# One step of a hybrid attention layer on one core: modulation product, w_out loads, last gate and prompt moved

## The chip, the cores and the metric

The kernel runs on 1 core of one Trainium2 chip. The metric is device time in microseconds of one execution. Of the engines, TensorE (PE) multiplies, VectorE (DVE), ScalarE (ACT) and GpSimd (POOL) work on tiles, and SyncE (SP) issues most of the DMA transfers. Each engine takes its instructions in a fixed order.

## The reference

```python
def merge_out(o_a, g_a, o_b, g_b, w_out):
    return jnp.concatenate([o_a * jax.nn.silu(g_a), o_b * jax.nn.silu(g_b)], axis=-1) @ w_out
...
shift, scale, gate = modulation(c, w_mod[l], b_mod[l])      # silu(c) @ w_mod + b_mod, in thirds
h = rmsnorm(xs, norm_gain[l]) * (1.0 + scale) + shift
q_a, k_a, v_a, g_a, q_b, k_b, v_b, g_b = project(h, w_in[l], ...)
...                                                         # axial rotary positions on q and k
o_a = global_attn_latent(q_a, k_a, v_a, cache_k_a[:, l], cache_v_a[:, l])
o_b = window_attn_latent(q_b, k_b, v_b, cache_k_b[:, l], cache_v_b[:, l], sink_b[l])
xs = xs + gate * merge_out(o_a, g_a, o_b, g_b, w_out[l])
```

One layer, float32. There are 1024 latent tokens and 128 prompt tokens of width 1024. Mixer A is global attention (8 query heads, 2 key heads, head size 64) over 1024 latent and 128 cached keys; mixer B takes a window of 128 on either side, the cached keys and a sink. The prompt goes through the same weights with a modulation of its own and attends to itself alone. Outputs are both residual streams and the prompt's keys and values.

## The kernel before, in words

Nearly every product is made of float32 values split into a high and a low part, so that three fast products (high by high, high by low, low by high) stand for one exact one. The work goes through stages:

1. **Start.** Nine tiles of 128 tokens are loaded (`load_x`), normed (`norm`: square on ACT, then two small instructions for the inverse root), scaled on DVE (`scaled`), transposed on TensorE (`turned`, L432), modulated to h (ACT and DVE, `modulated`) and split. The modulation's rows are a product on TensorE for each of 8 slices j of w_mod (`modulate_rows`, L398), copied (L401), transposed (`modulate`, L407) and added up to a scale and a shift. `warm(n)` issues n dummy matmuls (L468) between real ones; the tuple `WARM` has the counts. Tiles 1 to 4 are turned first, into one bank, and the first gate products (L273, L274, L269) follow with weights split by `W_GA.split()` (L244, L246).
2. **Projections** of queries, keys, values and gates. Queries and gates go out to DRAM (`qd`, `gd`) and are read again per unit (`u_load`, `load_gate`). The last gate of mixer B is not made by the Silu table but by `put_quotient`, in four steps, each in a tick of its own from `QUOTIENT_AT`: exponential, logarithm, exponential (ACT), product (DVE).
3. **Attention.** The work is a list of units (token tile t, mixer m, key head g), 32 of latents and then 4 of the prompt (32 to 35). Each unit has one slot for each block of 128 keys (a prompt's unit is padded to two slots). In slot s the program issues `tick()` (what is due on the agenda), the scores of slot s, loads and other items due, some matmuls of the output projection from a queue (`outq`), and the values product of slot s - 3 (`LAG`). So the order of each engine's instructions is that in which the slots and ticks issue them; `in_order` fixes it.
4. **Ends of a unit.** Counted in ticks from its last values product: `inverse` (ACT, L1207 to L1210), `gated` (DVE L1219, from the bank of PSUM into one third of the tile `spare`, the third being the unit's number modulo 3; then POOL L1221 by the gate `sgl`), `parts` (ACT L1231 high part; POOL L1233 low part a tick later), and for mixer B the output products (L1266). The ticks are `END_AT`, `EDGE_END` (global units of the first and last latent tile), `PROMPT_END`. `gated` also sets `load_gate(i + 2)` on the agenda, `GATE_LATE` ticks later. The values product has two banks, the `sgl` tiles have two buffers.
5. **w_out** comes in 16 blocks of 128 x 512, each loaded and split in two. Blocks 0 to 10 come during the last gates (`WO_STEPS`), the last five during the attention (`WO_LATE`: block, slot of its load; three ticks later `split_wo` on ACT L1088 and POOL L1089). These five use the two buffers `yt`, which the last gate's quotient has before and the output's sums behind them.

Of the kernel before, what the change touches and what calls it, by code (L numbers as in the profile page):

```python
# [33 lines left out]
PROMPT_AT = 32  # L34
# [12 lines left out]
PH_DVE = 0  # L47
MX_END = 10
MX_LEAD = 3
QUOTIENT_AT = 8  # L50
EARLY_STEPS = 50
SPLIT_LAG = 2

WO_LATE = {12: 18, 13: 19, 11: 30, 14: 31, 15: 33}

WO_STEPS = ((0, 4, 4), (1, 5, 5), (2, 6), (3, 7), (4, 8, 6), (5, 9), (6, 11), (7, 12, 10), (8, 13), (9, 14), (10, 16))
TURN = 2
# [1 line left out]
PAD = 2  # L59
X_FROM = 1  # L60
SECOND_FROM = 5
WARM = (4, 3, 3, 5, 2, 7)
WIDE = 5
LOADLEAD = 5
OUTRATE = 2.5
# [6 lines left out]
GATE_LATE = 2  # L72
END_AT = (1, 4, 6, 9)
EDGE_END = (1, 3, 6, 9)
PROMPT_END = (2, 4, 5, 7)
QTS = 5
PROMPT_LEAD = 4
EX_AT = (2, 2, 5)
# [37 lines left out]
def hybrid_step(ctx, tc, x_prompt, x_sample, cache_k_a, cache_v_a, cache_k_b, cache_v_b,  # L116
# [17 lines left out]
    def later(n, f):  # L134

        agenda.setdefault(now[0] + n, []).append(f)
# [208 lines left out]
    with tc.tile_pool(name="st", bufs=2, side="right") as st:  # L345
# [85 lines left out]
        def turned(px, j, t):  # L431
            nc.tensor.transpose(px, xn[t][:, P * j : P * j + P], ident)  # L432
# [32 lines left out]
        def warm(n):  # L465

            for _ in range(n):
                nc.tensor.matmul(small[0], ident_b, ident_b.unsqueeze(1).to_broadcast([P, 4, P]), start=True, stop=True)  # L468
# [20 lines left out]
        for j in range(KT + 2):  # L489
            if j == 0:  # L490
                px = bank_tr("px0_1")
                norm(1, nc.vector)
                norm(2, nc.vector)
                conditions()
                for i in range(4):
                    if 0 < i < 3:
                        norm(2 + i, nc.vector)
                    scaled(1 + i, rx.pop(1 + i))
                    warm(WARM[i])
                    turned(px[:, P * i : P * i + P], 0, 1 + i)  # L500
                modulate_rows(0)
                W_GA.split()
                warm(WARM[4])
                modulate(0)
                modulated(px, 0, 1, 4, 0)
                warm(WARM[5])
                continue
            big_on, small_on = j <= KT, 2 <= j
            if j < KT:
                W_GA.split()  # L510
            if j == 1:
                load_wm(3)
                norm(5)
            if big_on:
                first_gates(0, j - 1, 0)
                first_gates(1, j - 1, 0)
            if j < KT:
                modulate_rows(j)
                if j + 3 < KT:
                    load_wm(j + 3)  # L520
                if X_FROM <= j < X_FROM + 3:
                    load_x(rest[j - X_FROM])
            if big_on:
                first_gates(0, j - 1, 1)
                first_gates(1, j - 1, 1)
            if j == KT:
                sg_tile.append(lambda n: st.tile([P, D], F32, name="xn1", bufs=1)[:, 0:512])
                put_gates(big[0], 0, 0, slice(0, 512), nc.sync)
            if j == 1:
                modulate(1)  # L530
                scaled(5, rx.pop(5))
                transposed(1, 1, 4, 0)
                norm(6)
                first_gates(2, 0)
                first_gates(3, 0)
            elif j == 2:
                scaled(6, rx.pop(6))
                px5 = bank_tr("px01_5")
                for i in range(4):
                    turned(px5[:, P * i : P * i + P], i // 2, 5 + i % 2)  # L540
                modulate(2)
                for i in range(2):
                    modulated(px5[:, 256 * i : 256 * i + 256], i, 5, 2, 0)
                first_gates(2, 1)
                transposed(2, 1, 4, 0)
                first_gates(3, 1)
                transposed(2, 5, 2, 0)
            else:
                if big_on:
                    first_gates(2, j - 1)  # L550
                if j < KT:
                    modulate(j)
                    transposed(j, 1, 4, 0)
                if big_on:
                    first_gates(3, j - 1)
                if j < KT:
                    transposed(j, 5, 2 if j < WIDE else 4, 0)
            if X_FROM + 1 < j <= X_FROM + 4:
                t = rest[j - X_FROM - 2]
                scaled(t, rx.pop(t))  # L560
            if X_FROM < j <= X_FROM + 3:
                norm(rest[j - X_FROM - 1])
            for ch in range(4):
                if small_on:
                    next_gates(ch, j - 2)
                if ch % 2 or j >= KT:
                    more()
            if KT - 2 <= j < KT:
                raw = st.tile([P, KT, 2, P], F32, tag="wm", name=f"raw_qa{j}", bufs=3).rearrange(
                    "p (k a) s n -> p k (a s n)", a=2)  # L570
                k0 = 4 * (j - KT + 2)
                c0, n = W_QA.cols[0]
                nc.sync.dma_start(
                    raw, w_in[P * k0 : P * k0 + 512, c0 : c0 + n].rearrange("(k p) n -> p k n", p=P))
                W_QA.raw += [raw[:, k] for k in range(4)]
# [48 lines left out]
    with tc.tile_pool(name="qt", bufs=2, side="right") as qt:  # L624
# [89 lines left out]
        for m in range(2):  # L714
            w, nxt = ((W_QA, W_QB), (W_QB, W_KV))[m]
            ts = list(range(1, NT)) + [0]
            for t in ts:
# [3 lines left out]
                if (m, t) in ((0, ts[-2]), (1, ts[GATE_AT[0]])):  # L721
                    n = len(wg) // 2
# [465 lines left out]
    def values(i, b, last, blk, ph, pl):  # L1188
        t, m, g = units[i]
        _, vh, vl = blk  # L1190
        if b == 0:
            pvb[i] = bank("C", f"pv{i}")
        pv = pvb[i]
        two = vh.rearrange("p s d -> p (s d)")
        nc.tensor.matmul(pv, two, ph, start=(b == 0), stop=False)  # L1195
        if m == 0:
            nc.tensor.matmul(pv[0:64, :], vl, ph, start=False, stop=False)  # L1197
        nc.tensor.matmul(pv, two, pl, start=False, stop=last)  # L1198
        if not last:
            return  # L1200

        v = {}

        def inverse():
            v["rs"] = w2.tile([64, 512], F32, tag="rs", name=f"rs{i}", bufs=1)
            if m == 1:
                nc.scalar.copy(v["rs"], pv[64:128, :])  # L1207
                return
            nc.scalar.activation(v["rs"], pv[64:128, :], AF.Ln)
            nc.scalar.activation(v["rs"], v["rs"], AF.Exp, scale=-1.0)  # L1210

        def gated():
            rs = v["rs"]
            o = 768 + 256 * (i % 3)
            of = spare[:, o : o + 256].rearrange("p (c n) -> p c n", c=2)
            pvv = pv[0:64, :].rearrange("p (c s n) -> p c s n", s=2, n=P)
            srv = rs.rearrange("p (c s n) -> p c s n", s=2, n=P)
            for s in range(2):
                nc.vector.tensor_tensor(of[64 * s : 64 * s + 64], pvv[:, :, s, :], srv[:, :, s, :],  # L1219
                                        op=ALU.add if m else ALU.mult)  # L1220
            nc.gpsimd.tensor_tensor(of, of, sgl.pop(i), op=ALU.mult)  # L1221
            later(GATE_LATE, lambda: load_gate(i + 2))
            v["of"] = of

        def parts():
            while held[0] == NOG:
                outq.pop(0)()
            held[0] += 1
            oh = ogp.tile([P, 2, P], F32R, tag="ogh", name=f"ogh{i}")
            ol = ogp.tile([P, 2, P], F32R, tag="ogl", name=f"ogl{i}")  # L1230
            nc.scalar.copy(oh, v["of"])  # L1231
            og[t, 2 * m + g] = oh, ol
            later(1, lambda: nc.gpsimd.tensor_tensor(ol, v["of"], oh, op=ALU.subtract))  # L1233

        ends = (EDGE_END if m == 0 and t in (1, NL) else END_AT) if t else PROMPT_END
        for n, f in zip(ends, (inverse, gated, parts)):
            later(n, f)
        if m == 1:
            later(ends[3], lambda: outq.extend(out_items(t, g)))
# [54 lines left out]
    for i, (t, m, g) in enumerate(units):  # L1294
        if i in EARLY:
            continue
        if m == 0:
            items, done = max_items(i)
            at, end = [start[i - 2] + a for a in (MX_AT if i > 2 else MX_FIRST)], start[i - 2] + MX_END
# [19 lines left out]
    for s in range(len(slots) + LAG + PROMPT_END[3]):  # L1319
        tick()  # L1320
        if s < len(slots):
            live.append((slots[s], slots[s] and scores(slots[s][0], slots[s][1], slots[s][3])))
        for n, at in WO_LATE.items():
            if s == at:
                load_wo(n, w2)
                later(3, lambda n=n: split_wo(n, True))
        for f in due.get(s, ()):
            f()
        rate = (OUTRATE if s < start[PROMPT_AT - 2] else LASTRATE) if s < start[PROMPT_AT] else PADRATE
        credit = min(credit + rate, 6.0) if outq else 0.0  # L1330
        while outq and credit >= 1.0:
            outq.pop(0)()
            credit -= 1.0
        if s >= LAG and live:
            slot, parts = live.pop(0)
            if slot:
                values(*slot, *parts)
# [65 lines left out]
```

## Time and profile before

| | |
|---|---|
| time, median of 3 runs | 711.9 us (711.27 to 711.98) |
| the profiled execution's own time | 711.62 us |
| its span, first to last instruction | 709.8 us |
| mean granted TensorE clock | 0.999 |
| TensorE busy | 694.6 us (98%) |
| VectorE busy | 454.4 us (64%) |
| ScalarE busy | 414.0 us (58%) |
| GpSimd busy | 335.7 us (47%) |

A row of a timeline has the start in us from the span's start, the duration in us (of the whole run of equal instructions where it ends in xN), the engine, the line of the kernel, the operation, out<-in by the names of tiles, the shapes, and in brackets how long the engine stood idle ahead of it and what released it. A row of the waits has engine, tile and line, what it waited for, the total in us, the number of times and the longest. TensorE's matmuls overlap: one of 512 columns is shown with about 0.4 us.

### The profile page before, as it was taken

The numbers are of one execution on the slowest core, as the hardware profiler recorded it, in microseconds if no ns is written. First come the engines' busy times: TensorE is split into PE (matmuls) and PEld (weight loads), VectorE is DVE, ScalarE is ACT, GpSimd is POOL, SyncE is SP. The second block draws the span as 40 slices with busy tenths as digits, with TensorE's granted clock in tenths as the row PEclk, the third lists the DMA queues.
The fourth block names the chain that finished last, engine by engine and source line by source line (L and its number), as shares of the span: only waits on it lengthen the run. The fifth ranks groups of instructions, "written<-read, shape, count | busy, mean of one in ns | idle before, by whom it ended". The sixth has DMA issues, their size and how long they took to land. (4 is left out here: it accounts for less than half of the span.)

```text
span 709.8 us, 10658 instructions
## 1 busy us (share of the span) xinstructions
PE 694.6 (98%) x3524; PEld 557.6 (79%) x3524; DVE 454.4 (64%) x1010; ACT 414.0 (58%) x835; POOL 335.7 (47%) x349
## 2 busy tenths in 40 slices
PE   6999999999999999999999999999999999999997
PEld 2778988877788889976778788888888888887775
DVE  3575247867577763566667577667676775776562
ACT  4546412421324441188877877787788778877860
POOL 2466023233223330255867655755575557555751
PEclk9999999999999999999999999999999999999999
DMA  9951381228234026422222122122221231212323
GB/s 346 399 192 65 115 303 75 91 104 282 105 127 125 3 74 185 142 78 87 67 91 82 32 82 74 48 80 61 82 72 41 68 89 45 83 53 89 91 80 121
DMA packets 53304, 78.58 MB, mean 111 GB/s; under 512 B 6584, under 2 KB 25464, under 8 KB 52352
## 3 DMA queue, kind: packets, MB, share of 16 engines
q1 hardware_dynamic: 45936, 66.92, 28.8%
q10 hardware_dynamic: 7312, 10.98, 4.1%
q8 instruction: 28, 0.46, 0.3%
q14 instruction: 28, 0.23, 0.1%
HBM read 58.69 MB, written 19.18 MB: 110 GB/s over the span
## 5 line engine op out<-in xcount | busy, mean ns | idle before, releaser
L1185 POOL TENSOR_TENSOR pl<-pe,ph 128x512 fp32r<-128x512 f32 x130 | 167.5, 1291 | 149.7 <-ACT ph L1181 70.2
L933 DVE TENSOR_REDUCE mx<-pmx 128x1 f32<-128x384 f32 x192 | 101.0, 552 | 59.4 <-PE pmx L932 58.2
L1177 ACT ACTIVATE pe<-st 128x512 f32<-128x512 f32 x146 | 86.7, 594 | 29.3 <-PE st L1175 28.8
L1181 ACT CAST ph<-pe 128x512 fp32r<-128x512 f32 x146 | 90.6, 621 | 4.9
L1195 PE MATMUL pv<-ph,v_hi 128*128 128x512 f32 x208 | 82.5, 397 | 1.5 <-DVE spare L1219 1.5
L1198 PE MATMUL pv<-pl,v_hi 128*128 128x512 f32 x208 | 82.4, 396 | 0.0
L1266 PE MATMUL po<-wo,ogh 128*128 128x512 f32 x216 | 73.1, 395 | 0.2 <-DVE yt L1275 0.2
L184 POOL TENSOR_TENSOR rs_q<-ms_q,mhalf 128x8 f32<-128x8 f32 x18 | 34.8, 1933 | 81.0 <-DVE ms_q L182 81.0
L993 DVE CUSTOM_DVE_ANT_0 sn<-sn,mask,nsink 128x512 f32<-128x512 f32 (+1 forms) x64 | 46.4, 724 | 38.8 <-PE sn L990 35.8
L932 PE MATMUL pmx<-kha,qt 128*128 128x384 f32 x192 | 61.7, 367 | 0.6 <-ACT pen L979 0.3
L1174 PE MATMUL st<-qt,kha 128*128 128x512 f32 x144 | 57.9, 402 | 0.8 <-DVE pl L1171 0.8
L1197 PE MATMUL pv<-ph,v_lo 128*64 128x512 f32 x146 | 57.7, 395 | 0.0
L1175 PE MATMUL st<-qb,kla 68*128 68x512 f32 x144 | 57.0, 396 | 0.0
L1198 PEld LDWEIGHTS pv<-pl,v_hi 128*128 128x128 f32 x208 | 39.2, 189 | 16.7 <-POOL pl L1185 0.2
L698 ACT CAST qo0q<-ptq 128x512 fp32r<-128x512 f32 x18 | 10.6, 587 | 65.8 <-PE ptq L695 59.9
L979 ACT ACTIVATE pen<-sn,nm 128x512 f32<-128x512 f32 (+2 forms) x72 | 44.9, 625 | 5.9 <-DVE nm L1006 2.7
L1170 ACT CAST ph<-st 128x512 fp32r<-128x512 f32 x62 | 36.4, 587 | 19.8 <-PE st L1169 19.0
L1195 PEld LDWEIGHTS pv<-ph,v_hi 128*128 128x128 f32 x208 | 39.3, 189 | 8.5 <-ACT ogh L1231 1.1
L1266 PEld LDWEIGHTS po<-wo,ogh 128*128 128x128 f32 x216 | 40.0, 188 | 6.8 <-DVE yt L1275 0.6
L1171 DVE TENSOR_TENSOR pl<-st,ph 128x512 fp32r<-128x512 f32 x62 | 42.4, 685 | 2.3 <-ACT ph L1170 1.7
L1266 PE MATMUL po<-wo,ogl 128*128 128x512 f32 x108 | 42.6, 394 | 0.0
L932 PEld LDWEIGHTS pmx<-kha,qt 128*128 128x128 f32 x192 | 35.5, 190 | 9.0 <-DVE mx L933 3.3
(230 smaller groups left out, 1699.9 us busy)
## 6 DMA issues: line engine op xcount, KB each, us to landing
qt<-qd SPq DMA_DIRECT2D x72, 128.0 KB, 2.9
wm<-in_w_mod_ss_dram SPq DMA_DIRECT2D x7, 1024.0 KB, 9.4
qd<-qo0q ACTq DMA_DIRECT2D x18, 256.0 KB, 2.4
sgl<-gd SPq DMA_DIRECT2D x36, 128.0 KB
out_dram<-yt SPq DMA_DIRECT2D x17, 256.0 KB, 2.0
xn<-in_x_sample_dram SPq DMA_DIRECT2D x8, 512.0 KB
wg<-in_w_mod_g_dram SPq DMA_DIRECT2D x4, 1024.0 KB, 8.7
wraw<-in_w_out_dram SPq DMA_DIRECT2D x16, 256.0 KB, 4.9
```

What stands on the lines that cost most here:

```text
L932: nc.tensor.matmul(pm[:, 0:384], lhs, kha[:, g, 3 * b : 3 * b + 3, :], start=True, stop=True)
L933: nc.vector.tensor_reduce(mx[:, h, b : b + 1], pm[:, 0:384], axis=AX.X, op=ALU.max)
L993: nc.vector.tensor_tensor_reduce(s, s, mask[:, m0 : m0 + n], -1.0, nsink[:, 4 * g + h : 4 * g + h + 1], op0=ALU.add, op1=ALU.min, accum_ou ...
L1174: nc.tensor.matmul(s, kh, qtile[i], start=True, stop=False)
L1175: nc.tensor.matmul(s, kl, qbtile[i], start=False, stop=True)
L1177: nc.scalar.activation(pe, s, AF.Exp)
L1181: nc.scalar.copy(ph, pe)
L1185: nc.gpsimd.tensor_tensor(pl, pe, ph, op=ALU.subtract)
L1195: nc.tensor.matmul(pv, two, ph, start=(b == 0), stop=False)
L1197: nc.tensor.matmul(pv[0:64, :], vl, ph, start=False, stop=False)
L1198: nc.tensor.matmul(pv, two, pl, start=False, stop=last)
L1266: nc.tensor.matmul(po[n], a, wo_parts[KT * n + k][lo], start=(k == KS[0] and p == 0), stop=(k == KS[-1] and p == 2))
```

## The change

- `modulate_rows(0)` is issued ahead of the fourth transpose (i == 3) and no longer behind it; the dummies go from (4, 3, 3, 5, 2, 7) to (7, 2, 3, 2, 2, 6).
- `norm(6)` is issued right behind `norm(5)`, ahead of the first gate products of j == 1, and no longer behind tile 1's second h write.
- The four steps of the last gate's quotient come one tick sooner.
- w_out's blocks 11 and 14 are loaded in slots 28 and 29 (30 and 31 before) and split three ticks later; block 15 is loaded in slot 32 (33) and split four ticks later, so in tick 36 as before. Blocks 12 and 13 are as they were.
- All four steps at a prompt unit's end come one tick sooner, and the gate loads of units 32 to 35 one tick behind `gated` and not two.

```diff
-QUOTIENT_AT = 8
+QUOTIENT_AT = 7
...
-WO_LATE = {12: 18, 13: 19, 11: 30, 14: 31, 15: 33}
+WO_LATE = {12: (18, 3), 13: (19, 3), 11: (28, 3), 14: (29, 3), 15: (32, 4)}
...
-WARM = (4, 3, 3, 5, 2, 7)
+WARM = (7, 2, 3, 2, 2, 6)
...
-PROMPT_END = (2, 4, 5, 7)
+PROMPT_END = (1, 3, 4, 6)
...
                     scaled(1 + i, rx.pop(1 + i))
                     warm(WARM[i])
+                    if i == 3:
+                        modulate_rows(0)
                     turned(px[:, P * i : P * i + P], 0, 1 + i)
-                modulate_rows(0)
                 W_GA.split()
                 warm(WARM[4])
                 modulate(0)
...
                 norm(5)
+                norm(6)
...
                 transposed(1, 1, 4, 0)
-                norm(6)
...
-            later(GATE_LATE, lambda: load_gate(i + 2))
+            later(GATE_LATE if i + 2 < PROMPT_AT else 1, lambda: load_gate(i + 2))
...
-        for n, at in WO_LATE.items():
+        for n, (at, wait) in WO_LATE.items():
             if s == at:
                 load_wo(n, w2)
-                later(3, lambda n=n: split_wo(n, True))
+                later(wait, lambda n=n: split_wo(n, True))
```

## The prediction, on record before the changed kernel ran

> **What bounds the kernel now.** I read the page's busy shares first, then TensorE's waits, then the timelines of the places where TensorE waits, and last those of the engines that release it.
>
> ```profile
> span 709.8 us, 10658 instructions
> PE 694.6 (98%) x3524; PEld 557.6 (79%) x3524; DVE 454.4 (64%) x1010; ACT 414.0 (58%) x835; POOL 335.7 (47%) x349
> ```
>
> TensorE (PE) is busy for 694.6 of 709.8 us; no other engine is over 64%. So a change is worth only what it takes from, or adds to, the places where TensorE's stream of matmuls stands still. Its own waits say where these are:
>
> ```profile
> PE pg_s L468 <- DVE ident_b L349: 5.3, 1, 5.3
> PE px L432 <- DVE xn L418: 1.6, 2, 1.1
> PE pv L1195 <- DVE spare L1219: 1.5, 2, 0.8
> ```
>
> The first 5.3 us wait for the identity, which the change leaves alone. The second is the start (token tiles not yet scaled), the third the end (prompt). These lists leave out one thing: in the first 17 us TensorE is busy with dummies, which count as work here and are none. The gain of an earlier start is read from when the first real product begins, not from idle time.
>
> **The start: modulation product ahead of the fourth transpose, other dummies, norm(6) sooner.** Rows of TensorE, then the scaling of the fourth tile on VectorE (DVE), then ScalarE (ACT), then the DMA rate in slices of 1.5 us from 0 to 60 us:
>
> ```profile
> 8.50 1.49 PE L468 MATMUL pg_s<-ident_b 128*128 128x512 bf16 x3
> 9.78 0.42 PE L432 MATMUL px<-ident,xn 128*128 128x128 f32 x1
> ...
> 13.13 1.07 PE L398 MATMUL pm<-wm,sil 128*32 128x256 f32 x16
> ...
> 14.75 0.44 PE L407 MATMUL pm<-ident,mrows 128*128 128x128 f32 x2
> 15.03 1.67 PE L468 MATMUL pg_s<-ident_b 128*128 128x512 bf16 x7
> 16.78 0.50 PE L273 MATMUL pg_f<-h,whiga 128*128 128x512 f32 x1
> ...
> 25.05 0.55 PE L432 MATMUL px<-ident,xn 128*128 128x128 f32 x3 [0.51 <-DVE xn L418]
> ...
> 32.42 0.38 PE L407 MATMUL pm<-ident,mrows 128*128 128x128 f32 x2
> ```
>
> ```profile
> 10.95 0.75 DVE L418 TENSOR_SCALAR xn<-xn,rsx 128x1024 f32<-128x1024 f32 x1 [0.44 <-POOL rsx L428]
> ```
>
> ```profile
> 12.27 0.62 ACT L244 CAST whiga<-rawga 128x512 fp32r<-128x512 f32 x1 [2.63 <-DMA rawga<-in_w_in_dram]
> ...
> 20.75 0.78 ACT L447 ACTIVATE h<-px,b_col,a_mod 128x512 fp32r<-128x512 f32 x1 [2.46 <-DVE b_col L413]
> ...
> 29.13 1.06 ACT L424 ACTIVATE sq<-xn 128x1024 bf16<-128x1024 f32 x1 [0.61 <-DMA xn<-in_x_sample_dram]
> 30.18 0.60 ACT L244 CAST whiga<-rawga 128x512 fp32r<-128x512 f32 x1
> ...
> 31.29 0.37 ACT L401 COPY mrows<-pm 128x256 f32<-128x256 f32 x1 [0.50 <-PE pm L398]
> ```
>
> ```profile
> GB/s 0 200 416 397 421 287 320 434 426 401 415 451 412 407 442 437 437 362 438 429 401 227 388 401 377 96 273 386 137 14 191 404 102 0 23 343 333 11 0 0
> ```
>
> A dummy takes about 0.43 us early (three from 8.50 to 9.78) and 0.25 us later (seven from 15.03 to 16.78): the clock comes up near 12 us. Seven dummies from 5.27 at 0.43 us end at 8.26, so the gap ahead of the first transpose closes and TensorE is busy without a break from 5.27. I take it that the faster pitch comes by about 9.5 us. The third tile is scaled 0.44 us ahead of the row of 10.95; its transpose is done near 10.8, two dummies near 11.3, and the 16 instructions of the product (1.07 us) begin. Their weight's second half must be there: rawga's first tile, 256 KB behind it in SyncE's queue, lands at 12.25 or so; at some 420 GB/s that is 0.6 us later, so the half lands near 11.6 and the product ends near 12.2, against 14.2 before. The fourth tile is scaled at 11.70; its transpose and two dummies fit while DVE copies the rows. The transposes of 14.75 come at 12.95, the first gate product of 16.78 at 15.0: **-1.8 us**. The two dummies fewer (24 to 22) are inside that.
>
> What is late next? norm(6) moves on ACT from behind the h write of 20.75 to ahead of it: a square of 1.06 us, as at 29.13, and a short read. Its x6 stands behind rawga, 1 MB of wm, rawga and x5: 2.36 MB from 12.25 at about 430 GB/s is 17.8 us, so the norm holds ACT until 19.0, when the write is wanted at 18.95: 0.1 us lost, -1.7. Its two small POOL instructions are moved past nothing. In return the wait of 0.51 us at 25.05 is covered: -1.7 to -1.9. Then the gain meets a landing: at 29.13 ACT waited for x7, and behind it in ACT's order stand the weight cast of 30.18 and the row copy of 31.29. SyncE's order of loads is unchanged and the rate row shows the queue full up to there, so x7 comes no sooner. The copy can follow the cast at 30.8, ends at 31.15, and the transposes of 32.42 come at 31.2: **-1.2 us**, which I take; ends: -1.8 (x7 a little sooner) and -0.4 (clock late). By the Trainium skill, "DMA: Bandwidth & Descriptors", section on queues, rings and completion order, each engine consumes one queue's descriptors in ring order, so x7 could not overtake; by it the sum stays at -1.2 and the -1.8 is out. The trace's landing at 29.1 agrees.
>
> **The last gate's quotient a tick sooner.** ACT and TensorE at that place:
>
> ```profile
> 318.77 0.52 ACT L316 ACTIVATE quotient<-quotient 128x384 f32<-128x384 f32 x1
> ```
>
> ```profile
> 321.17 0.23 PE L951 MATMUL ptm<-ident_r,m_nat 128*4 128x128 f32 x1 [0.16 <-DVE mx L933]
> ```
>
> Three ACT instructions, one DVE product and one store by SyncE move one slot up. On DVE the product now comes ahead of the small maxima of the slot before, where it has idle time; the reductions that TensorE waits for stand behind it in DVE's order and come about 0.2 us sooner, and the wait at 321.17 shrinks: **-0.2 us** (0.2 either way at the ends: on ACT an exponential is half a us later, three slots ahead of its use).
>
> **The late w_out loads.** SyncE, ACT, POOL, DVE, TensorE, and of the chain that ended last the output products, for the pitch:
>
> ```profile
> 364.16 0.33 SPq L1072 DMA_DIRECT2D wraw<-in_w_out_dram  x1
> ```
>
> ```profile
> 367.19 0.62 ACT L1088 CAST wo_big<-wraw 128x512 fp32r<-128x512 f32 x1 [1.59 <-DMA wraw<-in_w_out_dram]
> ```
>
> ```profile
> 362.84 1.29 POOL L1089 TENSOR_TENSOR wo<-wraw,wo 128x512 fp32r<-128x512 f32 x1
> ```
>
> ```profile
> 369.74 0.69 DVE L1171 TENSOR_TENSOR pl<-st,ph 128x512 fp32r<-128x512 f32 x1 [1.35 <-ACT ph L1170]
> ```
>
> ```profile
> 370.58 0.47 PE L1174 MATMUL st<-qt,kha 128*128 128x512 f32 x1 [0.40 <-DVE pl L1171]
> ```
>
> ```profile
> 688.24 5.48 PE po L1266 x24
> ```
>
> Here is a chain to be had: w_out block 15 can't be loaded until POOL has split block 11 in the same buffer (362.84 + 1.29, issue at 364.16); it lands 3.0 us later, ACT stands 1.59 us for it, the cast of the scores behind it is late, DVE is late, and TensorE waits at 370.58 (0.40 us idle; at a pitch of 5.48 / 24 = 0.23 the matmul before, 0.4 us long, would have been followed 0.16 sooner than its end, so some 0.55 is lost). Block 11 is now split two slots sooner, near 361.2; 15 is issued then, lands near 364.4, and its split, in the same slot as before, finds it there. The wait goes: **-0.55 us**. Two ACT casts (0.62 each) and POOL splits (1.29 each) come into slots 31 and 32; ACT had gaps there, and POOL's splits of the exponentials, pushed by 1.3 to 2.2 us, still come about 1 us ahead of their matmuls. Ends: -0.6 and +0.2.
>
> **The prompt's steps and its gate loads a tick sooner.** TensorE, ACT, POOL, DVE at the end:
>
> ```profile
> 684.68 0.47 PE L1266 MATMUL po<-wo_big,ogl 128*128 128x512 f32 x1
> 685.92 0.47 PE L1195 MATMUL pv<-ph,v_hi 128*128 128x512 f32 x1 [0.77 <-DVE spare L1219]
> ...
> 687.54 0.47 PE L1195 MATMUL pv<-ph,v_hi 128*128 128x512 f32 x1 [0.69 <-DVE spare L1219]
> ```
>
> ```profile
> 682.05 0.60 ACT L1177 ACTIVATE pe<-st 128x512 f32<-128x512 f32 x1 [0.63 <-PE st L1175]
> ...
> 683.63 0.60 ACT L1209 ACTIVATE rs<-pv 64x512 f32<-64x512 f32 x1
> ```
>
> ```profile
> 683.38 1.29 POOL L1185 TENSOR_TENSOR pl<-pe,ph 128x512 fp32r<-128x512 f32 x1 [1.94 <-ACT ph L1181]
> 684.62 0.74 POOL L1221 TENSOR_TENSOR spare<-spare,sgl 128x256 f32<-128x256 f32 x1
> 685.31 0.73 POOL L1233 TENSOR_TENSOR ogl<-spare,ogh 128x256 fp32r<-128x256 f32 x1
> ...
> 687.71 0.74 POOL L1221 TENSOR_TENSOR spare<-spare,sgl 128x256 f32<-128x256 f32 x1 [0.97 <-DMA sgl<-gd]
> 688.41 1.43 POOL L1233 TENSOR_TENSOR ogl<-spare,ogh 128x256 fp32r<-128x256 f32 x2
> ```
>
> ```profile
> 685.80 0.69 DVE L1171 TENSOR_TENSOR pl<-st,ph 128x512 fp32r<-128x512 f32 x1
> 686.55 0.85 DVE L1219 TENSOR_TENSOR spare<-pv,rs 64x256 f32<-64x256 f32 x2
> ```
>
> Unit 32's inverse (logarithm and exponential on ACT, 683.63) moves ahead of unit 34's exponential (682.05). It begins at 681.6, its result is there at 682.8, DVE reads unit 32's bank by 684.5, and the wait of 0.77 us at 685.92 goes. But TensorE then only reaches the next wait sooner: unit 35's product needs unit 33's bank, read at 686.55. What sets that read? Unit 34's exponential is 0.8 us later, and with it POOL's 683.38 and, in order behind it, the gate product of unit 31 (684.62, now 685.4 to 686.2). Unit 32's gate product (0.74 too), a tick sooner, now stands ahead of unit 30's low part (685.31), which so ends near 687.55 in place of 686.05. Unit 33's read writes the third of "spare" that unit 30's low part still reads (30 and 33 leave the same remainder by 3), so it goes from 686.55 to 687.6, and TensorE's 687.54 to 688.6: **+1.05 us**. Behind it stand only output products, so nothing takes it back. The unit 31 low part, now third behind unit 33's gate product (687.71, whose gate load followed the row of 684.62 and landed 2.3 us behind it, so not before 688.5 now), is ready near 690.7, just ahead of the ninth output product at 691.0. Ends: -0.2 (the low part still ends in time: pairing 685.80 + 0.69 with the read) and +1.2. The gate loads are alone in SyncE's queue there; a tick changes nothing.
>
> **Sum:** -1.2 - 0.2 - 0.55 + 1.05 = -0.9 us on the profiled 711.62 us (span 709.8): 710.7. The runs' median is 711.9, 0.3 above the profiled one: **711.0 us**.
>
> **Rivals.**
> 1. *The prompt's steps lose nothing.* If unit 30's low part stays ahead on POOL, the end gives -0.2 and the sum is -2.15: 709.75. For it: both waits at the end are on exactly the step that moves. Against it: the order on POOL follows from the ticks.
> 2. *x7 does not hold the start.* The -1.75 us reach the first gates whole: sum -1.45, 710.45. For it: ACT's wait there is only 0.61 us. Against it: the full queue.
> 3. *The middle does nothing*: quotient and w_out stay hidden or their waits go to the next in line: sum -0.15, 711.75.
> 4. *Slower: the clock comes up late.* There are now fewer dummies between the transposes. If the fast pitch is not there by 12.1 us, all up to the product run at 0.43: the third transpose at 11.2, two dummies to 12.1, the product at half speed to 14.1, transpose and two dummies to 15.3, against 14.75: +0.5 in place of -1.2. Sum +0.8: 712.7. It decides where the product starts on the slow clock; up at 12.1 as before, the start still gains 0.9. By the Trainium skill, "TensorE: Matmul & The Clock Gate", Parts 1 and 4, the clock is released after a busy window of some 3.4 us that runs free of the program, and transposes do not count as busy in the same way: by it the step could fall anywhere up to a window later, the case of this rival. The trace agrees only that the pitch changed near 12 us, after steady work from 8.2.
>
> **How the numbers follow.** Chances: as worked out 0.52 (711.0; its own range 710.3 to 711.7), rival 1 0.18, rival 2 0.10, rival 3 0.13, rival 4 0.07. A measurement tells about 0.2% (1.4 us) from no change: faster is below 710.5, slower above 713.3. Rival 1, half of rival 2 and a fifth of the first case (0.11) give faster 0.34; rival 4's upper part and an unforeseen wait 0.07 slower; the rest 0.59. The range, 709.4 to 712.7, goes from rival 1 to rival 4.
>
> **What would show it.** Start: first gate product at 15.0, ACT's square of x7 still at 29.1, the transposes at 31.2 behind it. Middle: no wait of TensorE near 369, ACT's cast of block 15 without a DMA wait. End: the first wait for "spare" gone, the second longer, with POOL's low part of unit 30 late ahead of it. The prediction is wrong if x7 lands with the shift, if the low parts keep their places on POOL, or if the product of 13.13 runs at the slow pitch.

## The result

| | median us | runs | ratio to before, 95% interval |
|---|---|---|---|
| before | 711.94 | 4 (711.27 to 712.39) | |
| after | 715.62 | 4 (714.89 to 716.33) | 1.0052 (1.0035 to 1.007) |

The change makes the kernel 3.7 us slower (2.5 to 5.0 by the interval); 711.0 was predicted, with a range up to 712.7. All of the loss arises in the last 30 us of the profile: one and the same values product of TensorE stands at 680.64 before and at 679.19 in the changed kernel, 1.45 us sooner, and yet the span is 713.2 us against 709.8. First the page of the changed kernel and TensorE's waits (total, times, longest):

```profile
span 713.2 us, 10654 instructions
PE 695.6 (98%) x3522; PEld 558.1 (78%) x3522; DVE 455.7 (64%) x1010; ACT 414.8 (58%) x835; POOL 334.8 (47%) x349
```

```profile
PE pv L1196 <- DVE spare L1220: 2.5, 1, 2.5
PE pv L1196 <- ACT ph L1182: 1.2, 1, 1.2
...
PE pv L1199 <- POOL pl L1186: 0.6, 1, 0.6
```

The two waits for `spare` (0.77 and 0.69 us) have become one of 2.5, and two waits for unit 34's exponential and its low part (`ph`, `pl`) are new. The lines are one further on than before from L499 on.

**The start** (timeline of the changed kernel, TensorE, then ScalarE):

```profile
11.26 1.07 PE L398 MATMUL pm<-wm,sil 128*32 128x256 f32 x16
...
15.26 0.50 PE L273 MATMUL pg_f<-h,whiga 128*128 128x512 f32 x1 [0.65 <-ACT h L447]
...
31.07 0.44 PE L407 MATMUL pm<-ident,mrows 128*128 128x128 f32 x2 [0.56 <-ACT mrows L401]
```

```profile
29.08 1.06 ACT L424 ACTIVATE sq<-xn 128x1024 bf16<-128x1024 f32 x1 [2.63 <-DMA xn<-in_x_sample_dram]
...
30.65 0.36 ACT L401 COPY mrows<-pm 128x256 f32<-128x256 f32 x1
```

The modulation product begins at 11.26, the first gate product comes 1.52 us sooner, x7 lands where it did, and the transposes behind it stand at 31.07 in place of 32.42: 1.35 us are gained there, and the instructions behind keep 1.3 us of it up to 300 us. In the windows of this profile the granted clock reads 1.00 from the first microsecond on, although a dummy takes 0.43 us up to about 10 us (seven in 3.17 us from 5.25); so for the start the pitch of the matmuls is the evidence of the clock, and not that column.

**The end** (timelines of ScalarE, POOL, VectorE and TensorE):

```profile
682.37 0.60 ACT L1210 ACTIVATE rs<-pv 64x512 f32<-64x512 f32 x1 [2.39 <-DVE spare L1220]
...
683.66 0.60 ACT L1178 ACTIVATE pe<-st 128x512 f32<-128x512 f32 x1
684.29 0.62 ACT L1182 CAST ph<-pe 128x512 fp32r<-128x512 f32 x1
```

```profile
684.98 1.28 POOL L1186 TENSOR_TENSOR pl<-pe,ph 128x512 fp32r<-128x512 f32 x1 [4.71 <-ACT ph L1182]
686.22 1.41 POOL L1222 TENSOR_TENSOR spare<-spare,sgl 128x256 f32<-128x256 f32 x2
687.59 0.73 POOL L1234 TENSOR_TENSOR ogl<-spare,ogh 128x256 fp32r<-128x256 f32 x1
```

```profile
681.40 0.86 DVE L1220 TENSOR_TENSOR spare<-pv,rs 64x256 f32<-64x256 f32 x2
...
688.35 0.85 DVE L1220 TENSOR_TENSOR spare<-pv,rs 64x256 f32<-64x256 f32 x2 [1.20 <-POOL ogl L1234]
```

```profile
683.30 0.48 PE L1267 MATMUL po<-wo_big,ogl 128*128 128x512 f32 x1
684.96 0.50 PE L1196 MATMUL pv<-ph,v_hi 128*128 128x512 f32 x1 [1.17 <-ACT ph L1182]
685.30 0.39 PE L1198 MATMUL pv<-ph,v_lo 128*64 128x512 f32 x1
686.31 0.50 PE L1199 MATMUL pv<-pl,v_hi 128*128 128x512 f32 x1 [0.62 <-POOL pl L1186]
689.34 0.71 PE L1196 MATMUL pv<-ph,v_hi 128*128 128x512 f32 x1 [2.53 <-DVE spare L1220]
```

Unit 32's inverse (682.37) is now first in ScalarE's order but stands 2.39 us: it writes the tile `rs`, of which there is one buffer, and that is free only when VectorE has read unit 31's reciprocals out of it (681.40 + 0.86 = 682.26). Behind it in order stand unit 34's exponential (683.66, 3.0 us later than 682.05 less 1.35) and its cast; POOL's low part waits for them, unit 31's and 32's gate products and unit 30's low part stand behind that, and VectorE's read of unit 33 writes the third of `spare` that unit 30's low part reads. And TensorE's clock falls (windows: us, TensorE busy, granted clock, DMA):

```profile
684.00:688.00 4.00, 1.23 (x3) 1.00 0.00 0
688.00:690.00 2.00, 0.66 (x2) 0.85 0.47 131
690.00:692.00 2.00, 2.00 (x7) 0.50 0.35 90
692.00:694.00 2.00, 2.00 (x9) 0.79 0.71 238
```

0.85 over 2 us is 0.6 us at half clock, 0.79 is 0.84 us: half clock from 689.4 to 692.84, 3.44 us. The eight matmuls in it follow at 0.43 us in place of 0.23, which costs 1.6 us. A wait costs the distance between two starts less the usual 0.23: 683.30 to 684.96, 685.30 to 686.31 and 686.31 to 689.34 give 1.43 + 0.78 + 2.80 = 5.0 us, a tenth more with the next matmul. The same sum for the changed kernel with the old ticks (a1 below; 683.43 to 684.71 and 685.25 to 686.33) is 1.05 + 0.85 = 1.9. So in these profiles the new ticks cost 3.2 us in waits and 1.6 in the clock, 4.8 together.

### The profile page after: what moved, and what is told of

It is laid out like the page before. It is cut to its first block, busy times and chain, and to the rows that moved or that the text cites. A ratio compares the mean times of both kernels' runs of the same rounds, so it can differ in the third digit from the quotient of the medians.

```text
span 713.2 us, 10654 instructions
## 1 busy us (share of the span) xinstructions
PE 695.6 (98%) x3522; PEld 558.1 (78%) x3522; DVE 455.7 (64%) x1010; ACT 414.8 (58%) x835; POOL 334.8 (47%) x349
```

## The experiments

| run | kernel | median us | ratio to before |
|---|---|---|---|
| a1 | after, old prompt ticks | 710.58 | 0.9977 (0.9967 to 0.9986) |
| a2 | before, new prompt ticks | 717.42 | 1.0073 (1.0057 to 1.0088) |
| a3 | after, only the inverse sooner | 714.37 | 1.0031 (1.0019 to 1.0044) |
| a4 | after, only the other three sooner | 713.19 | 1.0016 (1.0007 to 1.0025) |
| b1 | after, own room for `rs` | 712.94 | 1.0011 (1.0001 to 1.002) |
| b4 | b1, own room for unit 33's output | 710.97 | 0.9991 (0.9982 to 1.0) |
| b2 | after, 12 dummies in the gap | 713.58 | 1.0030 (1.0018 to 1.0043) |
| b3 | before, new start alone | 710.11 | 0.9976 (0.9967 to 0.9984) |
| c3 | before, new dummies alone | 710.83 | 0.9984 (0.9975 to 0.9993) |
| c4 | before, new order alone | 711.37 | 0.9993 (0.9983 to 1.0002) |
| c2 | b3 and the quotient | 710.33 | 0.9981 (0.9971 to 0.999) |
| c1 | b3 and w_out | 710.46 | 0.9980 (0.9971 to 0.9989) |
| d3 | b3, prompt's inverse sooner with room | 710.62 | 0.9983 (0.9974 to 0.9992) |
| d4 | d3, residual loads ahead of gate loads | 709.36 | 0.9967 (0.9954 to 0.9979) |

Before had a median between 711.8 and 712.1 in each set of runs, so medians of different sets are compared below to some 0.2 us at best. An interval of the ratio is about 0.002 wide, which is 1.4 us, and smaller differences are read from the places in the profiles.

### Whose loss is it: the prompt's ticks (a1 to a4)

```diff
-PROMPT_END = (1, 3, 4, 6)
+PROMPT_END = (2, 4, 5, 7)     # a1; a3: (1, 4, 5, 7); a4: (2, 3, 4, 6)
```

a2 is the kernel before with (1, 3, 4, 6) and the gate loads' tick.

> The changed kernel with the prompt's four steps at their old ticks (2, 4, 5, 7); the rest of the change stays, the tick of the prompt's gate loads too. Theory 1 (the prompt's steps lose all of it: unit 32's inverse stands on ScalarE for the one buffer of the reciprocals, and TensorE then falls to half its clock): 715.6 - 4.8 = about 710.4 to 710.8, with the two small waits for the third of spare back at 684.6 and 686.2 and all output products at 0.23 us. Theory 2 (the clock at the end falls because of the new dummies or an earlier start, and the ticks are innocent): 714 to 715.6, with slow matmuls near 689.

> The kernel before with the prompt's four steps a tick sooner and its gate loads a tick sooner, nothing else. Theory 1: +4.8, so 716.7 (715 where the clock holds). Theory 2: +1 (as predicted for the order on POOL alone), 713.

> The changed kernel with only the first of the four steps (the inverse) a tick sooner: 1, 4, 5, 7. Theory 1 (the inverse waits on ScalarE until unit 31's read frees the one buffer of the reciprocals): the wait of 2.4 us at rs stays, unit 34's exponential is late, about 712.4, up to 714 if the clock drops as well. Theory 2 (the order of the gate product and the low parts on POOL costs the time): no loss, 710.4.

> The changed kernel with the inverse at its old tick and the other three steps a tick sooner: 2, 3, 4, 6. Theory 1: ScalarE does not wait for rs, 710.4 or a little less. Theory 2: the low part of unit 30 stands behind the gate product of unit 32 on POOL, +0.75, 711.2 or more.

The prompt's ticks make the whole loss: without them the rest of the change is 1.5 us faster than before (a1), with nothing else they cost 5.3 (a2). The tick of the gate loads is in a1 too, so it isn't that. Of a2's surplus over the 4.8 the clock has a part: its windows

```profile
688.00:690.00 2.00, 0.54 (x1) 0.66 0.00 0
690.00:692.00 2.00, 0.64 (x2) 0.50 0.45 131
692.00:696.00 4.00, 4.00 (x12) 0.57 0.49 163
```

show half clock for 1.36 + 2 + 3.44 = 6.8 us, twice as long as in the changed kernel. But 2.7 us of it fall into the wait itself, which ends at 691.36; slow matmuls follow for 4.1 us in place of 3.5, which is some 0.3 us more. a3 keeps the wait for `rs`, as theory 1 said:

```profile
682.09 0.60 ACT L1210 ACTIVATE rs<-pv 64x512 f32<-64x512 f32 x1 [2.28 <-DVE spare L1220]
```

It comes out a little above the upper end that theory 1 gave (714.37 against 714), and the clock drops in it too. a4 has no such wait, so theory 1 expected 710.4; theory 2 said 711.2 or more from an addition of 0.75. 713.19 is far over the first and over twice that addition. Its ScalarE shows a third mechanism (first the two rows of a4, then the same copy in a1):

```profile
685.47 0.41 ACT L1232 CAST ogh<-spare 128x256 fp32r<-128x256 f32 x1 [1.13 <-POOL spare L1222]
685.90 0.58 ACT L1208 COPY rs<-pv 64x512 f32<-64x512 f32 x1
```

```profile
684.65 0.58 ACT L1208 COPY rs<-pv 64x512 f32<-64x512 f32 x1 [0.35 <-DVE spare L1220]
```

With `parts` a tick sooner and the inverse not, the high part of a gated tile, which waits for POOL's gate product, stands ahead of unit 33's copy on ScalarE. The copy is 1.25 us later, so is unit 33's read (686.58 against 685.34 on VectorE), and TensorE's second wait grows from 0.7 to 1.9. A further wait of 1.15 at 694.93 stands behind unit 35's read in VectorE's order. The order on POOL that theory 2 named is there too, but the low part of unit 30 ends at 686.13 and unit 33's copy at 686.48, so the copy decides. Moving steps together costs other things than moving them alone; a3 and a4 do not add up.

### The two shared buffers (b1, b4)

```diff
+            if t == 0 and m == 0:
+                if not room:
+                    room.append(qp2[0].tile([P, 4, 512], F32, tag="pen", name="room"))
+                v["rs"] = room[0][0:64, g, :]
+            else:
                 v["rs"] = w2.tile([64, 512], F32, tag="rs", name=f"rs{i}", bufs=1)
...
+            if i == PROMPT_AT + 1:                                       # b4 only
+                of = room[0][:, 2, 0:256].rearrange("p (c n) -> p c n", c=2)
```

(The expectation says units 32 and 33; the units with an inverse, whose reciprocals get the room, are 32 and 34.)

> The changed kernel, but the reciprocals of the prompt's units 32 and 33 go to a room of their own, so that unit 32's inverse need not wait until unit 31's read is done. Theory 1 (that wait is the greater part of the loss): the 2.4 us on ScalarE ahead of rs are gone, unit 34's exponential is 0.8 us late, what stays is near the +1.05 that was predicted, 711.5 to 711.8, and the clock holds. Theory 2 (the loss is the order on POOL): 715 or more as in the changed kernel.

> As the kernel with a room for the reciprocals of units 32 and 33, and unit 33's output tile in that room too, so that it need not wait until unit 30's low part is read. Theory 1 (the third of spare is what is left of the loss, as predicted): 0.3 to 0.8 under the kernel with the room alone, about 711. Theory 2 (other order on POOL, the low part of unit 31): no less than that kernel.

b1, timelines of ScalarE, VectorE and TensorE, then its windows:

```profile
680.70 0.60 ACT L1216 ACTIVATE room<-pv 64x512 f32<-64x512 f32 x1
...
681.99 0.60 ACT L1179 ACTIVATE pe<-st 128x512 f32<-128x512 f32 x1
```

```profile
686.70 0.85 DVE L1226 TENSOR_TENSOR spare<-pv,rs 64x256 f32<-64x256 f32 x2 [0.99 <-POOL ogl L1240]
```

```profile
684.71 0.45 PE L1200 MATMUL pv<-pl,v_hi 128*128 128x512 f32 x1
687.70 0.59 PE L1197 MATMUL pv<-ph,v_hi 128*128 128x512 f32 x1 [2.54 <-DVE spare L1226]
```

```profile
688.00:690.00 2.00, 2.00 (x6) 0.50 0.21 52
690.00:692.00 2.00, 2.00 (x7) 0.67 0.85 272
```

The wait on ScalarE is gone, and with it 2.7 us. b1 is what the prediction described: the first wait for `spare` gone, the second longer because unit 30's low part stands between. TensorE's stream loses 2.76 us at that place against 1.90 in a1, +0.9, where +1.05 was predicted. The rest, some 1.5 us between the medians, is the clock, which falls after this one wait too: half clock for 3.4 us by the windows. b4 takes the shared third of `spare` away, the longest wait falls to 1.4, the clock holds, and 2.0 more come back, not the 0.3 to 0.8 expected: the expectation left the clock out. That its "about 711" was met is luck, since it was counted from a time for b1 that was too low by more than a us. With both buffers out of the way the new ticks still gain nothing: b4 stands at 710.97, a1 with the old ticks at 710.58.

### The clock (b2)

```diff
+            if slot and slot[0] == NU - 1:
+                dummy = bank("A", "dummy")
+                for _ in range(12):
+                    nc.tensor.matmul(dummy, ident_b, ident_b.unsqueeze(1).to_broadcast([P, 4, P]), start=True,
+                                     stop=True)
```

> The changed kernel with 12 dummy products of 512 columns ahead of unit 35's values product, where TensorE stands for 2.5 us. Theory 1 (TensorE's clock falls to half because of the idle time in there, and that costs 1.5 to 1.7 us of the 4.8): the matmuls from 689.3 on keep a pitch of 0.23, about 714.0. Theory 2 (the clock falls for another reason, so idle time is not the cause): half speed stays, 715.6 or more.

```profile
688.00:690.00 2.00, 2.00 (x10) 1.00 0.46 131
690.00:692.00 2.00, 2.00 (x11) 1.00 0.25 69
```

Twelve matmuls that compute nothing make the kernel 2.0 us faster (713.58 against 715.62): the wait is as long as it was (686.51 to 689.55 between the two real matmuls, 686.31 to 689.34 without dummies), but the matmuls behind it keep their 0.23 us. So idle time is the cause of the low clock. How much is enough: in the profiled executions a wait of 2.54 us with nothing else (b1) was; 0.81 and 1.88 with three matmuls between (a4) were not, nor 1.4 (b4).

A profile is one execution, however, and the mean granted clock, which is on record for every run, says that runs of one kernel differ here. Five of a4's ten runs have 0.996 and no run of a1 or b3 is under 0.998, so in these five the clock very likely fell, though the profiled one (712.66, clock 0.999) shows nothing of it. Two of b1's ten runs have 1.000 (711.51 and 712.79), so there it very likely held in spite of the wait. The changed kernel's own runs are two at 0.998 (714.89 and 714.98, the profiled one) and two at 0.994 (716.27 and 716.33). So the clock's 1.6 us are the price in one execution and not a constant. What share of such a stretch must be idle is left open.

The Trainium skill, "TensorE: Matmul & The Clock Gate", Part 1, says that the clock is decided in free-running windows of about 3.4 us and halves after an idle one. The lengths agree: 3.44 us of half clock in the changed kernel, 6.8 in a2. Its rule that only gaps above some 3.4 us matter does not hold here: 2.54 us in b1 were enough.

### The start (b3, c3, c4)

b3 has only the start's part of the change; c3 only the dummies; c4 the order of product and norm with the old dummies.

> The kernel before with the changes at the start alone (modulation product ahead of the fourth transpose, the other dummies, norm 6 sooner). Theory 1 (the start's 1.3 us are kept through the whole kernel): 710.6. Theory 2 (they are lost at a later landing or wait): 711.9.

> The kernel before with the new dummies alone (7, 2, 3, 2, 2, 6 in place of 4, 3, 3, 5, 2, 7), the modulation product still behind the fourth transpose. Theory 1 (half of the start's gain is the clock that comes up sooner, half is the product that no longer waits for the fourth tile): the product begins near 12.2 in place of 13.13, the transposes at 32.42 come 0.5 to 1.3 sooner because the landing of x7 caps the rest, about 711.0. Theory 2 (the dummies give nothing without the new order): 711.9.

> The kernel before with the new order at the start alone (product ahead of the fourth transpose, norm 6 sooner), the old dummies. Theory 1: the clock comes up near 12 as before, the product begins near 12.1 behind five dummies that run slowly, 1.0 sooner than before, and x7 caps what is kept: 710.8 to 711.3. Theory 2 (without the early clock nothing is gained, the rival of the prediction): 711.9 or slower.

The modulation product of c3, then that of c4:

```profile
12.03 1.07 PE L398 MATMUL pm<-wm,sil 128*32 128x256 f32 x16
```

```profile
12.69 1.07 PE L398 MATMUL pm<-wm,sil 128*32 128x256 f32 x16
```

It began at 13.13 before and at 11.62 in b3. c3 lies near its expectation. c4 is just over its own: the five slow dummies took longer than allowed for, the product came 0.4 us sooner, not 1.0, and against before the time can't be told from no change. Yet in both profiles the transposes behind x7 come 1.1 us sooner (31.32 and 31.31 against 32.42), close to b3's 1.53, though the products differ by 0.7: x7 lands at 28.9 to 29.2 in all of these profiles and caps what is kept. So in these two executions either half brings most of what x7 lets through. They are the fastest of ten in both cases (709.91 and 710.23), though. By the medians of each set the dummies bring 1.0 us and the order 0.5, which may be nothing, and both together (b3) 1.9; how the gain divides stays open.

### The middle (c1, c2)

c1 adds `WO_LATE` of the change to b3, c2 `QUOTIENT_AT = 7`.

> The kernel before with the changes at the start and the late w_out loads; quotient and prompt as before. It tells the two changes of the middle apart. Theory 1 (the quotient made the new wait near 313, w_out the one near 364): the shift stays at -1.4 to -1.5 through 314 and 320, drops by 0.5 near 364, comes back by 0.4 to 0.5 at 370, so w_out is worth 0 to -0.2 and the time is 710.0 to 710.3. Theory 2 (the wait near 364 comes from the quotient's sooner maxima): no drop near 364, and -0.5 as predicted, 709.6.

> The kernel before with the changes at the start and the quotient a tick sooner, w_out and prompt as before. Theory 1 (the quotient's exponential stands ahead of a penalty on ScalarE, TensorE waits near 313, and the shorter wait at ptm gives back less): the shift falls by 0.35 to 0.4 at 314, 0.1 comes back by 320, so 0.25 is lost: 710.4. Theory 2 (as predicted, 0.2 gained): 709.9, no new wait near 313.

Both times stand within 0.35 us of b3's 710.11, which is within the intervals. The places differ, though. c2, ScalarE and TensorE:

```profile
311.88 0.48 ACT L310 ACTIVATE quotient<-pg 128x384 f32<-128x384 f32 x1
312.25 0.57 ACT L980 ACTIVATE pen<-sn,nm 128x384 f32<-128x384 f32 x1
```

```profile
312.97 0.45 PE L933 MATMUL pmx<-kha,qt 128*128 128x384 f32 x1 [0.18 <-ACT pen L980]
```

The quotient's exponential now stands ahead of a penalty that frees the bank of the next maxima: the shift against before falls from -1.52 to -1.16 at 314; 0.1 is back by 317, the wait at `ptm` near 321 (0.16 before) is gone, as predicted, and -1.44 is there again at 360, where b3 has -1.41. c1, VectorE, POOL, TensorE:

```profile
362.18 1.33 DVE L947 TENSOR_SCALAR m_nat<-m 128x4 fp32r<-128x4 f32 x1
363.43 0.55 DVE L934 TENSOR_REDUCE mx<-pmx 128x1 f32<-128x384 f32 x1
```

```profile
362.20 1.29 POOL L1186 TENSOR_TENSOR pl<-pe,ph 128x512 fp32r<-128x512 f32 x1
```

```profile
364.03 0.44 PE L933 MATMUL pmx<-kha,qt 128*128 128x384 f32 x1 [0.41 <-DVE mx L934]
```

A VectorE instruction on 128x4 took 1.33 us and ended 0.02 us behind POOL's. In b3 it took 0.51 (from 362.25), and ended 0.02 behind another POOL instruction, which ended at 362.74. w_out's splits, moved on POOL, put a long POOL instruction beside it; the maxima behind it are late and TensorE loses 0.57 at 364 and 0.1 at the next start. The wait at 370 goes as predicted and gives 0.65 back: against before nothing is left. Against b3 there was less to gain from the start: with the old loads the two matmuls at that place start 0.53 us apart in b3, 0.80 before, and 0.23 where nothing waits.

### A version that is faster than both (d3, d4)

d3 is b3 with the inverse a tick sooner, the rooms of b4, unit 33's read two ticks sooner, and its gate product and high part later, behind the low parts of units 31 and 32. d4 also issues the last image tile's residual loads earlier:

```diff
-PROMPT_END = (2, 4, 5, 7)
+PROMPT_END = (1, 4, 5, 7)
...
+        if i == PROMPT_AT + 1:
+            ends = (1, 2, 6, 7)
...
+            if i == PROMPT_AT + 1:
+                later(3, lambda: nc.gpsimd.tensor_tensor(of, of, sgl.pop(i), op=ALU.mult))
+            else:
                 nc.gpsimd.tensor_tensor(of, of, sgl.pop(i), op=ALU.mult)
...                                                                      # d4 only
-            if n == 0 and k == KS[4] and p == 0:
+            if n == 0 and k == KS[0 if t == NL else 4] and p == 0:
```

> The kernel before with the changes at the start, and of the prompt's steps only the inverse a tick sooner, with a room of its own for the reciprocals of units 32 and 34 and for unit 33's output tile; unit 33's read two ticks sooner, its gate product on POOL behind the low parts of units 31 and 32. Theory 1 (the two shared buffers are all that stood against the sooner steps, and the order on DVE and POOL is the rest): the idle time of TensorE between 683 and 689, 1.9 us in the kernel before, falls to 0.5 to 1.0, so 708.8 to 709.3. Theory 2 (something else holds unit 35's product): no gain over the start alone, 710.1 or more.

> The kernel with the inverse a tick sooner and a room of its own, and the two loads of the last image tile's residual rows (yt) put ahead of the prompt's gate loads in SyncE's queue. Theory 1 (there VectorE waited for yt because its load stood behind a gate load that waits for unit 33's gate product; TensorE lost 1.28 at 692.42): yt is there in time, the wait falls to the 0.3 that the kernel before shows, so 1.0 less than that kernel: 709.2 to 709.6. Theory 2 (the output products wait for something else there, the low parts or the store): 710.6 as without it.

d3's TensorE, VectorE and SyncE:

```profile
692.42 0.70 PE L1280 MATMUL po<-wo,ogh 128*128 128x512 f32 x2 [1.12 <-DVE yt L1289]
```

```profile
691.58 0.69 DVE L1289 TENSOR_TENSOR yt<-po,yt 128x512 f32<-128x512 f32 x1 [1.44 <-issue]
```

```profile
684.61 3.83 SPq L1157 DMA_DIRECT2D sgl<-gd  x3
688.49 0.93 SPq L1261 DMA_DIRECT2D yt<-in_x_sample_dram  x2
```

The waits of 1.9 us between 683 and 689 fell to 0.9, as theory 1 said (the longest left is 0.28 for unit 33's read), but 1.28 were lost at 692.42, so the time, 710.62, missed theory 1's 708.8 to 709.3 and is no better than b3's. Unit 33's later gate product holds a `sgl` buffer, SyncE waits for it with a gate load, and the residual rows (`yt`) stand behind that load, so VectorE had to wait for them. With those loads ahead (d4) SyncE issues them at 675.91, the loss at that place is 0.2, and 709.36 is 2.7 us under before. It is also 0.75 under b3, but the intervals of the two ratios overlap, so that part is likely and not sure.

## Why the prediction was wrong

- **The start** (-1.2): right, in the mechanism as well as the size. Product at 11.26 (11.3 predicted), first gate product at 15.26 (15.0), x7 at 29.08 (29.1), transposes at 31.07 (31.2): -1.35. Rival 2 is out: x7 landed within 0.3 us of the same time in five profiles. That, and not the order of the queue on which the prediction leaned, is what rules the -1.8 out. Rival 4 is out too: the two dummies ahead of the product take 0.59 us together.
- **The quotient** (-0.2): nothing in the end, 0.36 lost first. The half a us that the sooner step takes on ScalarE was charged to an exponential alone and called harmless ("three slots ahead of its use"). The penalty that stands behind it in the same order, and frees a bank, had no term. The wait at `ptm` did shrink as forecast.
- **Late w_out loads** (-0.55): nothing. The wait at 370 went, as worked out. The step that failed is that the splits moved on POOL were weighed only by their own matmuls; a VectorE instruction that was held up by POOL had no term. The wait at 370 is also no fixed price: with the old loads in place it is 0.40 before, 0.52 in c2 and 0.25 in c3, and in b3 and c4 too short to be listed. So the middle did nothing, which is rival 3's case.
- **The prompt's steps** (+1.05): the failed step is "It begins at 681.6". What held it could be read in the profile before, VectorE and then ScalarE:

```profile
682.73 0.86 DVE L1219 TENSOR_TENSOR spare<-pv,rs 64x256 f32<-64x256 f32 x2
```

```profile
683.21 0.40 ACT L1231 CAST ogh<-spare 128x256 fp32r<-128x256 f32 x1
683.63 0.60 ACT L1209 ACTIVATE rs<-pv 64x512 f32<-64x512 f32 x1
```

  The read that frees `rs` ended at 683.59, the inverse began at 683.63: the old tick fitted it by 0.04 us and hid the wait entirely behind other work. In the changed kernel that read ended at 682.26 and the inverse began at 682.37, and unit 34's exponential came 3.0 us late and not 0.8. b1, in which this wait alone is taken away, is 2.7 us faster. The rest of the step held: b1 shows the predicted order on POOL and +0.9 for it. The second missing term is the clock, 1.6 us in the profile, which no part of the prediction gave to the end of the kernel; no rival had the end lose more than 1.2.
- Sum: start -1.35, middle about 0, waits +3.2, clock +1.6: +3.5, against +3.4 between the two profiled executions (714.98 and 711.62) and +3.7 between the medians.

## What to carry to other kernels

A step that is issued sooner can start no sooner than the last reader of the buffer it writes: before moving it, look up that reader's end, and where the two already touch (here 0.04 us), the step gains nothing and everything behind it on its engine waits with it. Price a new wait on TensorE of the length seen here, 2.5 us, with the half clock that may follow, and cover it with dummies if it can't be removed. Take away the buffer first, then the order, then the next queue: the buffers gave 4.7 us against the changed kernel (b1 and b4), the queue 1.3 (d3 to d4), and the version with all of it stands at 709.36.

## What was not expected of the hardware

- TensorE's clock halved at a single idle stretch of 2.54 us (b1), for 3.4 us; in a2, with three waits, for 6.8. Dummies in the gap kept it at 1.00 (b2). Runs of one kernel differ in it: b1's mean clock is between 0.996 and 1.000, a4's between 0.996 and 0.999.
- A VectorE instruction on 4 elements per partition (`m_nat`) took 0.50 to 0.51 us in two kernels and 1.31 to 1.33 in two others, and each time ended within 0.04 us of the end of the POOL instruction beside it. The Trainium skill, "SBUF — State Buffer", section "Who interferes with whom", describes an exclusive port pair of the two engines that is held for a whole instruction; these rows agree with it.
